# First ffn of an encoder layer: its first two hidden tiles by slices of channels, the first root's squares on VectorE, modulations as columns

## The chip, the cores and the metric

The kernel runs on one core of a Trainium2 chip. The metric is the device time in microseconds (us) of one execution. Names of the engines as in the profile: PE is TensorE (PEld its weight loads), DVE is VectorE, ACT is ScalarE, POOL is GpSimd, SP is SyncE, on whose queue nearly all loads are issued. Each engine runs its own instructions strictly in their order and waits for others by semaphores.

## The reference

A layer for 1024 tokens of 1024 channels: half a SwiGLU ffn, a mixer (latent attention and a recurrence), half an ffn again, a final norm. What this case touches is the beginning:

```python
c_act = jax.nn.silu(c)
mod = c_act @ w_mod[l] + b_mod[l]                  # 9 x 1024
sh1, sc1, gt1, ... = jnp.split(mod, N_MOD, axis=-1)
u = modulate(rmsnorm(h, ffn1_norm_g[l]), sh1, sc1) # u * (1 + scale) + shift
h = h + 0.5 * gt1[:, None, :] * swiglu(u, w_gate, w_up, w_down)
# rmsnorm: x * rsqrt(mean(x*x) + eps) * g;  swiglu: (silu(u @ w_gate) * (u @ w_up)) @ w_down
```

All in float32. The hidden width is 2816, 22 tiles of 128.

## The kernel before

Channels lie on the partitions, in 8 tiles of 128; tokens lie in the columns, in two halves of 512. `h[d][a]` is the stream's tile d in half a. A float32 product is made of three matmuls of a shorter type: each operand is split into a high part (a cast on ACT, L59) and a low part (a subtraction on DVE, L60), and `mm3` (L66) multiplies high by high, high by low, low by high. A pair of high and low part is called `pair` in the rows.

The opening of the first ffn is code in `tile_layer` and in `ffn`. `load_x` loads a half of the stream. `root(0)` squares the eight tiles on ACT and sums over channels on PE with a matrix of ones (L1644, L1645), so that the sum stands on every partition; `root_mean` (L252, L253) takes the square root on ACT and the reciprocal on DVE, 512 wide. `root(1)` goes by `SumSq` and `rstd`: squares on ACT, sums over tiles on DVE (L206, `nacc`), token sums on PE (L214), a root of four columns, and `spread` (L224, L228, L229), which lays it out on every partition, once in PSUM and once as a copy in SBUF (`nr`).

The shift and the gain of the first two tiles of channels are made on PE (`mod_first`, L150), as a row of 128 columns that is copied by ACT and turned into columns by small products (L158). Those of tiles 2 to 7 are made on DVE (`mod_one`, L138, twelve of them), each from a loaded weight tile `wmod` of 512 KB and the spread silu of c (`cact`). `gain` (L184) adds one and multiplies by the norm's weight.

`norm_raw` norms a tile: even tiles on DVE (L318) and then a shift on ACT (L319), odd tiles on POOL (L315) and then gain and shift on ACT (L316). Half 0 goes through `normed` and `stream_first`, half 1 through `second_half`.

The first two hidden tiles go by `up_plain`: 2 tiles x gate and up x 2 halves x 8 channel tiles x 3 = 192 matmuls (L66, sums `ps_w` in PSUM). All later ones go by seven products in place of eight (`products7`), for which `stream_sums` makes sums and differences of the two halves (L353) and splits them.

A scheduler puts every engine's instructions into an order when the program is built; the order of the code is its starting point. Short-lived tiles take slots in turn: `k.spare` (512 wide, squares) has four, `k.wide` (the `wmod` tiles) sixteen.

## Time and profile before

| | |
|---|---|
| time, median of 3 runs | 2127.43 us (2125.19 to 2128.57) |
| profiled execution, first to last instruction | 2127.5 us |
| PE, DVE, ACT, POOL busy | 96%, 73%, 43%, 12% |
| chain that ended last | PE 78%, DVE 13%, DMA 4%, others 5% |
| L66 products into `ps_w` (both ffns) | 3744, busy 876.8 us |

The profile has no other time for its execution than the span, which stands beside the median of the runs. The page is an overview; the rows below come from the timeline (start, duration, engine, line, operation, tiles, in brackets the idle time before it and what ended it), from windows (busy time of each engine in a stretch) and from groups (busy time and mean of a kind of instruction in a stretch).

### The profile page before, as it was taken

Reading aid. Unit: us, or ns where it says so; the run is one execution under the profiler, and the core shown is the slowest. Engines: PE = TensorE matmul, PEld = TensorE weight load, DVE = VectorE, ACT = ScalarE, POOL = GpSimd, SP = SyncE. Lnnn points to the kernel's source line nnn. Section 1 sums busy time; section 2 is a strip of 40 time slices with the busy share of each in tenths; the row PEclk is TensorE's granted clock in tenths of the full one; section 3 lists DMA queues with packets and bytes.
Section 4 is the critical chain, followed back from the end, with each engine's and each line's share of the span. In section 5 each row is a group of like instructions: output and inputs, shape, how many; then the busy total and the mean of one; then the engine's idle time right before and its main releaser. Section 6 shows DMA issues by size and latency. Waiting matters only on the chain.

```text
span 2127.5 us, 28417 instructions
## 1 busy us (share of the span) xinstructions
PE 2052.5 (96%) x10496; PEld 1649.7 (78%) x10496; DVE 1551.5 (73%) x2718; ACT 924.3 (43%) x1614; POOL 251.6 (12%) x259
## 2 busy tenths in 40 slices
PE   6999999999999999997989999999999999999998
PEld 4788878887888767766768887777888888878887
DVE  6999996579895677788865656566655556589975
ACT  5643343344342566652344443455433333454333
POOL 1100000000001254531142222111000000000001
PEclk8999999999999999999999999999999999999999
DMA  8277732235332124545336853551322222363322
GB/s 329 94 236 246 248 112 94 89 125 182 105 124 93 56 70 131 139 127 131 91 86 168 198 161 119 193 177 52 100 88 73 86 80 89 99 193 109 102 72 80
DMA packets 189771, 273.74 MB, mean 129 GB/s; under 512 B 77504, under 2 KB 121920, under 8 KB 189632
## 3 DMA queue, kind: packets, MB, share of 16 engines
q1 hardware_dynamic: 187920, 268.62, 40.5%
q0 software_dynamic: 1280, 3.15, 0.5%
q8 instruction: 83, 1.36, 0.3%
q14 instruction: 56, 0.46, 0.1%
q10 hardware_dynamic: 432, 0.15, 0.0%
HBM read 202.66 MB, written 66.58 MB: 127 GB/s over the span
## 4 chain that ended last, share of the span: by engine, by line
PE 78%; DVE 13%; DMA 4%; issue 2%; ACT 1%; SPq 1%; POOL 1%; DVEq 0%; ACTq 0%; POOLq 0%
PE ps_w L66 36%; PE ps_dn L66 20%; PE ps_in L66 5%; PE ps_wo L66 3%; DVE Tpr L1317 2%; DVE pair L60 2%; PE ps_ov L1230 2%; PE ps_z L1415 1%; PE ps_s L66 1%; PE ps_uq L66 1%; DVE T L1321 1%; PE ps_x L951 1%; PE ps_pt L1222 1%; PE ps_s L1198 1%; PE ps_y L1442 1%
## 5 line engine op out<-in xcount | busy, mean ns | idle before, releaser
L66 PE MATMUL ps_w<-pair 128*128 128x512 f32 x3744 | 876.8, 395 | 13.4 <-ACT pair L59 9.7
L66 PEld LDWEIGHTS ps_w<-pair 128*128 128x128 f32 x3744 | 704.7, 189 | 182.7 <-ACT pair L59 11.3
L66 PE MATMUL ps_in<-pair,win 128*128 128x512 f32 x960 | 253.2, 414 | 8.4 <-DVE acc L1069 4.1
L60 DVE TENSOR_TENSOR pair<-raw,pair 128x512 fp32r<-128x512 f32 x256 | 177.8, 703 | 109.0 <-ACT pair L59 108.9
L59 ACT CAST pair<-raw 128x512 fp32r<-128x512 f32 x256 | 155.4, 621 | 226.4 <-PE ps_w L66 178.4
L66 PE MATMUL ps_dn<-pair 128*128 128x512 f32 x1008 | 236.6, 393 | 3.1 <-DVE part L608 1.7
L66 PEld LDWEIGHTS ps_in<-pair,win 128*128 128x128 f32 x960 | 183.4, 194 | 59.2 <-issue 10.9
L66 PEld LDWEIGHTS ps_dn<-pair 128*128 128x128 f32 x1008 | 188.9, 188 | 47.9 <-DVE part L608 2.5
L66 PE MATMUL ps_dn<-pair,dh 128*128 128x512 f32 (+1 forms) x704 | 204.2, 375 | 0.0
L66 PEld LDWEIGHTS ps_dn<-pair,dh 128*128 128x128 f32 x704 | 128.1, 188 | 25.8 <-issue 0.7
L388 ACT COPY part<-ps_w 128x512 f32<-128x512 f32 x120 | 70.1, 585 | 166.6 <-PE ps_w L66 157.9
L66 PE MATMUL ps_dn<-pair,dl 128*128 128x512 f32 (+1 forms) x352 | 131.2, 375 | 0.0
L551 DVE SCALAR_TENSOR_TENSOR h<-ps_dn,mod,h 128x512 f32<-128x512 f32 (+1 forms) x128 | 90.6, 715 | 37.6 <-PE ps_dn L66 37.3
L59 ACT CAST pair<-hraw 128x512 fp32r<-128x512 f32 x124 | 73.4, 620 | 69.5 <-DMA hraw<-hidD 29.6
L206 POOL TENSOR_TENSOR nacc<-nacc,nsq 128x512 f32<-128x512 f32 x12 | 17.7, 1472 | 670.4 <-ACT nsq L202 670.4
L138 DVE SCALAR_TENSOR_TENSOR wmod<-wmod,cact 128x1024 f32<-128x1024 f32 x68 | 83.1, 1224 | 9.6 <-DMA wmod<-w_mod 9.3
L486 DVE TENSOR_TENSOR t<-ps_w,part 128x512 f32<-128x512 f32 x80 | 54.8, 691 | 46.5 <-PE ps_w L66 27.9
L60 DVE TENSOR_TENSOR pair<-hraw,pair 128x512 fp32r<-128x512 f32 x124 | 83.4, 689 | 5.9 <-ACT pair L59 5.6
L699 POOL TENSOR_TENSOR h<-h,nr 128x256 f32<-128x256 f32 (+1 forms) x6 | 5.4, 916 | 648.8 <-ACT nr L229 648.8
L66 PE MATMUL ps_wo<-pair,woh 128*128 128x512 f32 x256 | 80.0, 394 | 0.6 <-ACT woh L59 0.6
L66 PEld LDWEIGHTS ps_dn<-pair,dl 128*128 128x128 f32 x352 | 66.3, 188 | 12.9 <-issue 0.2
L481 DVE TENSOR_TENSOR c<-ps_w,part 128x512 f32<-128x512 f32 x80 | 53.5, 688 | 28.8 <-PE ps_w L66 23.5
(348 smaller groups left out, 3101.7 us busy)
## 6 DMA issues: line engine op xcount, KB each, us to landing
wmod<-w_mod SPq DMA_DIRECT2D x68, 512.0 KB, 4.4
raw<-ffn_w_gate SPq DMA_DIRECT2D x44, 512.0 KB, 3.6
raw<-ffn_w_up SPq DMA_DIRECT2D x44, 512.0 KB, 4.5
hidD<-c SPq DMA_DIRECT2D x44, 512.0 KB, 2.7
hraw<-hidD SPq DMA_DIRECT2D x44, 512.0 KB, 3.3
draw<-ffn_w_down SPq DMA_DIRECT2D x40, 512.0 KB, 3.7
h<-x SPq DMA_DIRECT2D x32, 256.0 KB, 4.8
hD<-h SPq DMA_DIRECT2D x32, 256.0 KB, 2.0
```

The lines of the kernel that those rows point to most:

```text
L59: k.nc.scalar.copy(out=hi, in_=src)
L60: k.nc.vector.tensor_tensor(out=lo, in0=src, in1=hi.bitcast(F32), op=ALU.subtract)
L66: k.nc.tensor.matmul(out, lhsT=x, rhs=y, start=start, stop=stop, skip_group_check=onto)
L138: k.nc.vector.scalar_tensor_tensor(out=w, in0=w, scalar=1.0, in1=k.cact, op0=ALU.mult, op1=ALU.mult, accum_out=m)
L388: nc.scalar.copy(out=t, in_=x)
L481: nc.vector.tensor_tensor(out=c[i][:, j], in0=x, in1=y, op=ALU.add)
L486: nc.vector.tensor_tensor(out=t, in0=x, in1=y, op=ALU.add)
L551: nc.vector.scalar_tensor_tensor(out=y, in0=x, scalar=gt[:, d : d + 1], in1=y, op0=ALU.mult, op1=ALU.add)
L951: nc.tensor.matmul(t[:, 2 * P * e : 2 * P * (e + 1)].rearrange("p (h s q) -> p h s q", s=2, q=L), lhsT=BK8[:, 2 * c + e, :], rhs=pad[:, 2 ...
L1198: nc.tensor.matmul(t[:, :mm], lhsT=r[high], rhs=k.kr[1, b][high, :mm], start=False, stop=True)
L1230: nc.tensor.matmul(x.po[:, cols], lhsT=pt[:, b * P : (b + 1) * P], rhs=k.v[b][:, cols], start=b == 0, stop=b == x.i)
L1317: nc.vector.tensor_tensor(out=v, in0=T[:, 0:t, 0:t].rearrange("p s c -> p c s"), in1=xp[:, 0:t, t][:, None, :].broadcast_to([P, t, t]), op ...
```

## The change

The first two hidden tiles of the first ffn go by `up_sliced`. It loads all four weight tiles first, then splits them, and takes the products by a table `SLICES` of (half, channel tiles, hidden tiles): tiles 0, 1 of half 0, tiles 2, 3 of half 0, tiles 0 to 3 of half 1 for the first hidden tile, and so on. A callback `feed(half, tile)` norms and splits a tile of the stream just before the first slice that needs it, and makes the second root when the first tile of half 1 is asked for. The first root goes the way of the second one (`SumSq` with sums on DVE, `rstd`). Both norms now take the root from its copy in SBUF. `mod_first` makes the columns directly, the weight tile as the stationary operand. `k.spare` has three slots, `k.wide` eight, and the second root's copy lies in the fourth slot.

```diff
 def mod_first(k, d, w):
     nc = k.nc
-    t = ps(k, "norm")
+    t = ps(k, "norm")[:, :2]
     for v in range(2):
         for i in range(ND):
             nc.tensor.matmul(
-                t[0:1, v * P : (v + 1) * P], lhsT=k.ccol[:, i : i + 1], rhs=w[v][:, i * P : (i + 1) * P],
+                t[:, v : v + 1], lhsT=w[v][:, i * P : (i + 1) * P], rhs=k.ccol[:, i : i + 1],
                 start=i == 0, stop=i == ND - 1,
             )
-    row = tmp(k, "row")[0:1, : 2 * P]
-    nc.scalar.copy(out=row, in_=t[0:1, : 2 * P])
-    t = ps(k, "norm")[:, :2]
-    for v in range(2):
-        nc.tensor.matmul(
-            t[:, v : v + 1], lhsT=row[:, v * P : (v + 1) * P], rhs=k.ones[0:1, 0:1], start=True, stop=True
-        )
...
+SLICES = (
+    (0, (0, 1), (0, 1)), (0, (2, 3), (0, 1)), (1, (0, 1, 2, 3), (0,)), (0, (4, 5), (0, 1)), (1, (4, 5), (0,)),
+    (0, (6, 7), (0, 1)), (1, (6, 7), (0,)), (1, tuple(range(ND)), (1,)),
+)
...
+    def up_sliced(f):
+        A, c = [], []
+        for i in range(2):
+            for w in (wg, wu):
+                raw = pool.tile([P, 2, HB], F32, name="raw", tag="raw", bufs=4)
+                nc.sync.dma_start(out=raw.rearrange("p a (d q) -> p (a d) q", q=P), in_=w[f + i])
+                A.append((raw, [pair(pool, "wo", 8) for _ in range(2)]))
+        start[0]()
+        for b in range(2):
+            for raw, blocks in A:
+                split(k, raw[:, b], *blocks[b])
+        c = [cell() for _ in range(2)]
+        sums, fed = {}, set()
+        for j, slices, which in SLICES:
+            for d in slices:
+                if (j, d) not in fed:
+                    fed.add((j, d))
+                    sliced(j, d)
+            for i in which:
+                for e in range(2):
+                    if (i, e, j) not in sums:
+                        sums[i, e, j] = ps(k, "w7")
+                    for d in slices:
+                        hi, lo = A[2 * i + e][1][d // 4]
+                        q = slice(d % 4 * P, (d % 4 + 1) * P)
+                        mm3(k, sums[i, e, j], hi[:, q], lo[:, q], *u["plain"][j][d], d == 0, d == ND - 1)
...
+        start[3]()
...
-        k.wide = spare(us)
-        k.spare = spare(fs[8:])
+        k.wide = spare(us[:8])
+        k.spare = spare(fs[8:11])
...
         def root(a):
-            if a:
-                ss = SumSq(k, pool, nc.vector)
-                for d in range(ND):
-                    ss.add(h[d][a])
-                r = rstd(k, pool, ss)
-                return r
-            t = ps(k, "norm")
+            ss = SumSq(k, pool, nc.vector)
             for d in range(ND):
-                sq = tmp(k, "nsq")
-                nc.scalar.activation(out=sq, in_=h[d][a], func=AF.Square)
-                nc.tensor.matmul(t, lhsT=k.ones, rhs=sq, start=d == 0, stop=d == ND - 1)
-            r = pool.tile([P, HB], F32, name="r", tag="nr", bufs=1)
-            root_mean(k, t, D, r)
-            return r, r
+                ss.add(h[d][a])
+            r.append([rstd(k, pool, ss, ("nr", "f11")[a])[1]] * 2)
...
+        def feed(a, d):
+            if a and not d:
+                root(1)
+            if not a and d >= early:
+                mods(d)
+            norm_raw(k, r[a], h[d][a], d, "ffn1_norm_g", 0)
+            split(k, h[d][a], *u["plain"][a][d])
```

How the built order changes, at three places. First ACT at the program's start, before; `raw` are weight tiles, `r` is the first root:

```order
L252 ACT_TABLE_LOAD
L252 ACTIVATE r_191<-ps_norm_166,eps_67 128x512
L59 CAST pair_244<-raw_242 128x512
L59 CAST pair_245<-raw_242 128x512
L155 COPY row_211<-ps_norm_194 1x256
L59 CAST pair_252<-raw_250 128x512
L59 CAST pair_253<-raw_250 128x512
L59 CAST pair_260<-raw_258 128x512
```

and with the change, where `nr_216` is the first root's copy:

```order
L245 ACT_TABLE_LOAD
L245 ACTIVATE rt_213<-ps_norm_204,eps_67 128x4
L59 CAST pair_261<-raw_259 128x512
L59 CAST pair_265<-raw_263 128x512
L59 CAST pair_269<-raw_267 128x512
L222 COPY nr_216<-ps_norm_218 128x512
L59 CAST pair_273<-raw_271 128x512
L59 CAST pair_262<-raw_259 128x512
```

The root of 512 columns stood ahead of all eight casts. Now a root of four columns stands there, and the copy of the spread root behind three casts.

Then DVE around the second root, before (`nr_420` is its spreading, `mod_77` the modulations, `pair_367` to `pair_369` tiles 5 to 7 of half 0, `raw_877` a weight tile of the next hidden tiles):

```order
L184 SCALAR_TENSOR_TENSOR gs_ffn1_norm_g_81<-mod_77,pv_140 128x1
L60 TENSOR_TENSOR pair_367<-h4_0_148,pair_367 128x512
L138 SCALAR_TENSOR_TENSOR wmod_314,mod_77<-wmod_314,cact_274 128x1024
L141 TENSOR_TENSOR mod_77<-mod_77,b_mod_141 128x1
L318 SCALAR_TENSOR_TENSOR h6_0_149<-h6_0_149,gs_ffn1_norm_g_81,r_191 128x512
L141 TENSOR_TENSOR mod_77<-mod_77,b_mod_141 128x1
L184 SCALAR_TENSOR_TENSOR gs_ffn1_norm_g_81<-mod_77,pv_140 128x1
L224 TENSOR_TENSOR nr_420<-ident_60,rt_417 128x512
L60 TENSOR_TENSOR pair_368<-h6_0_149,pair_368 128x512
L395 TENSOR_TENSOR s1_897<-raw_877 128x512
L60 TENSOR_TENSOR pair_369<-h6_0_149,pair_369 128x512
L374 TENSOR_TENSOR raw_877<-raw_875,raw_877 128x512
```

and with the change (`rt_444` is the second root before it is spread, which is the row after the last one here; `pair_146` is tile 6; `raw_744`, `s1_898`, `raw_878` belong to the next hidden tiles):

```order
L138 SCALAR_TENSOR_TENSOR wmod_305,mod_77<-wmod_305,cact_275 128x1024
L141 TENSOR_TENSOR mod_77<-mod_77,b_mod_157 128x1
L60 TENSOR_TENSOR pair_146<-h6_0_165,pair_146 128x512
L367 TENSOR_TENSOR raw_744<-raw_742,raw_744 128x512
L138 SCALAR_TENSOR_TENSOR wmod_315,mod_77<-wmod_315,cact_275 128x1024
L388 TENSOR_TENSOR s1_898<-raw_878 128x512
L141 TENSOR_TENSOR mod_77<-mod_77,b_mod_157 128x1
L177 SCALAR_TENSOR_TENSOR gs_ffn1_norm_g_81<-mod_77,pv_156 128x1
L246 RECIPROCAL rt_444<-rt_444 128x4
L141 TENSOR_TENSOR mod_77<-mod_77,b_mod_157 128x1
L367 TENSOR_TENSOR raw_878<-raw_876,raw_878 128x512
L177 SCALAR_TENSOR_TENSOR gs_ffn1_norm_g_81<-mod_77,pv_156 128x1
```

One sum (L388) and two differences (L367) of the next tiles' weights stand here ahead of the spreading, and another sum a few rows higher; the gain of tile 7 (the last row) stands directly before it.

Last PE at the passage from half 0 to half 1, before (`pair_368`, `pair_369` are tiles 6 and 7 of half 0; `pair_441`, `pair_442` tiles 0 and 1 of half 1):

```order
L66 MATMUL ps_w7_544<-pair_368,pair_269 128x512 x2
L66 MATMUL ps_w7_544<-pair_369,pair_269 128x512
L66 MATMUL ps_w7_466<-pair_369,pair_245 128x512 x2
L66 MATMUL ps_w7_491<-pair_369,pair_253 128x512 x2
L66 MATMUL ps_w7_519<-pair_369,pair_261 128x512 x2
L66 MATMUL ps_w7_544<-pair_369,pair_269 128x512 x2
L66 MATMUL ps_w7_571<-pair_441,pair_244 128x512
L66 MATMUL ps_w7_596<-pair_441,pair_252 128x512
L66 MATMUL ps_w7_571<-pair_441,pair_244 128x512 x2
L66 MATMUL ps_w7_571<-pair_442,pair_244 128x512
```

and with the change (`pair_146`, `pair_147` are tiles 6 and 7 of half 0; `pair_148`, `pair_149` tiles 0 and 1 of half 1):

```order
L66 MATMUL ps_w7_343<-pair_146,pair_262 128x512 x3
L66 MATMUL ps_w7_343<-pair_147,pair_262 128x512 x3
L66 MATMUL ps_w7_350<-pair_146,pair_266 128x512 x3
L66 MATMUL ps_w7_350<-pair_147,pair_266 128x512 x3
L66 MATMUL ps_w7_357<-pair_146,pair_270 128x512 x3
L66 MATMUL ps_w7_357<-pair_147,pair_270 128x512 x3
L66 MATMUL ps_w7_364<-pair_146,pair_274 128x512 x3
L66 MATMUL ps_w7_364<-pair_147,pair_274 128x512 x3
L66 MATMUL ps_w7_468<-pair_148,pair_261 128x512
L66 MATMUL ps_w7_481<-pair_148,pair_265 128x512
L66 MATMUL ps_w7_468<-pair_148,pair_261 128x512 x2
L66 MATMUL ps_w7_468<-pair_149,pair_261 128x512
```

In both orders the products of half 0 come before those of half 1. The spread of the second root stood ahead of tile 6's products and now stands ahead of tile 5's; with tile 5 (12 products) the rows of tiles 6 and 7 (24) are what is left of half 0 there.

## Rows read from the trace of the kernel before

**Rows 1.** Windows: us, busy us of PE, PEld, DVE, ACT, POOL, clock, DMA

```profile
20.00:30.00 10.00, 4.34 (x31) 3.22 (x30) 10.00 (x15) 5.96 (x9) 5.65 (x4) 0.75 1.03 400
...
40.00:50.00 10.00, 6.02 (x32) 4.77 (x30) 10.00 (x25) 4.83 (x8) 0.00 (x0) 0.78 0.70 276
...
70.00:80.00 10.00, 10.00 (x44) 8.04 (x43) 10.00 (x18) 8.63 (x16) 0.00 (x0) 1.00 0.00 0
```

**Rows 2.** Timeline, PE: start, us, instructions merged, idle before

```profile
65.58 34.78 PE L66 MATMUL ps_w<-pair 128*128 128x512 f32 x142 [2.03 <-DVE pair L60]
```

**Rows 3.** Groups of PE from 28.9 to 65.5: busy us, mean ns, idle before

```profile
L66 PE MATMUL ps_w<-pair 128*128 128x512 f32 x98 | 27.8, 439 | 10.0 <-ACT pair L59 9.7 <-DVE pair L60 0.2
```

**Rows 4.** Groups from 70 to 140

```profile
L66 PE MATMUL ps_w<-pair 128*128 128x512 f32 x304 | 70.6, 394 | 0.0
```

**Rows 5.** Timeline of the first root and the raw splits, 9 to 29

```profile
9.28 0.74 SPq L452 DMA_DIRECT2D raw<-ffn_w_gate  x1
...
10.10 0.63 ACT L1644 ACTIVATE nsq<-h 128x512 f32<-128x512 f32 x1 [0.23 <-PE ps_norm L1645]
...
13.58 1.28 ACT L252 ACT_TABLE_LOAD   x1 [2.85 <-PE ps_norm L1645]
...
15.60 3.35 DVE L253 RECIPROCAL r<-r 128x512 f32<-128x512 f32 x1 [15.60 <-ACT r L252]
...
18.87 2.30 DVE L60 TENSOR_TENSOR pair<-raw,pair 128x512 fp32r<-128x512 f32 x2
...
19.09 6.55 POOL L315 TENSOR_TENSOR h<-h,r 128x512 f32<-128x512 f32 x4 [17.08 <-DVE r L253]
...
21.16 3.36 DVE L60 TENSOR_TENSOR pair<-raw,pair 128x512 fp32r<-128x512 f32 x2
...
24.44 1.22 DVE L184 SCALAR_TENSOR_TENSOR gs_ffn_norm_g<-mod,pv 128x1 f32<-128x1 f32 x1
...
27.45 1.28 DVE L60 TENSOR_TENSOR pair<-raw,pair 128x512 fp32r<-128x512 f32 x2
```

**Rows 6.** Timeline of the second root, 42 to 57

```profile
42.86 0.28 PE L214 MATMUL ps_norm<-ones,nacc 128*128 128x1 f32 x2
...
44.34 0.36 PE L214 MATMUL ps_norm<-ones,nsq 128*128 128x1 f32 x2
...
44.73 0.26 ACT L252 ACTIVATE rt<-ps_norm,eps 128x4 f32<-128x4 f32 x1 [2.89 <-PE ps_norm L214]
...
54.02 0.69 DVE L224 TENSOR_TENSOR nr<-ident,rt 128x512 f32<-128x512 f32 x1
...
55.89 1.02 PE L228 MATMUL ps_norm<-nr,ones 128*128 128x512 f32 x2
```

**Rows 7.** Loads issued from 8.9 to 9.5: KB each, us to landing

```profile
raw<-ffn_w_gate SPq DMA_DIRECT2D x1, 512.0 KB, 10.3
```

**Rows 8.** Groups of DVE from 28.6 to 54

```profile
L138 DVE SCALAR_TENSOR_TENSOR wmod<-wmod,cact 128x1024 f32<-128x1024 f32 x12 | 14.6, 1221 | 0.0
L206 DVE TENSOR_TENSOR nacc<-nacc,nsq 128x512 f32<-128x512 f32 x6 | 4.1, 688 | 0.6 <-ACT nsq L202 0.4
L60 DVE TENSOR_TENSOR pair<-h,pair 128x512 fp32r<-128x512 f32 x6 | 4.1, 687 | 0.0
L318 DVE SCALAR_TENSOR_TENSOR h<-h,gs_ffn_norm_g,r 128x512 f32<-128x512 f32 x3 | 2.3, 750 | 0.0
```

**Rows 9.** Timeline of half 1's norm, 59 to 65

```profile
59.44 2.71 DVE L318 SCALAR_TENSOR_TENSOR h<-h,gs_ffn_norm_g,ps_norm 128x512 f32<-128x512 f32 x4
...
60.84 0.80 ACT L316 ACTIVATE h<-h,mod,gs_ffn_norm_g 128x512 f32<-128x512 f32 x1
...
62.07 2.85 DVE L353 TENSOR_TENSOR h<-h,h 128x512 f32<-128x512 f32 x3
62.16 0.60 ACT L59 CAST pair<-h 128x512 fp32r<-128x512 f32 x1
```

**Rows 10.** Window of the slow clock after the restart at 65.58

```profile
66.00:69.00 3.00, 3.00 (x9) 2.33 (x8) 3.00 (x6) 2.99 (x5) 0.00 (x0) 0.50 0.03 5
```

More of the change, by code (lines that the diff above doesn't have):

```diff
@@ L253, in root_mean, with rstd @@
     k.nc.vector.reciprocal(out=out, in_=out)
-def rstd(k, pool, ss):
+def rstd(k, pool, ss, tag="nr"):
     t = ps(k, "norm")
@@ L429, in ffn @@
 def ffn(
-    k, u, h, wg, wu, wd, gt, pool, groups, cells, start, turn, steps1, steps2, final, done, pieces, ahead=None
+    k, u, h, wg, wu, wd, gt, pool, groups, cells, start, turn, steps1, steps2, final, done, pieces, ahead=None,
+    sliced=None
 ):
```

36 lines of the change are left out of this document (15 added, 21 removed).

## The prediction

> **What bounds the kernel now.** I read the page first: PE is busy 96% of the span and has 78% of the chain that ended last. In the windows PE has no gap from about 70 us on [rows 1], so what the opening of the first ffn loses or wins is passed on whole to the end. In the same windows the opening itself: between 20 and 30 us PE is busy 4.34 us and between 40 and 50 it is 6.02, while DVE has 10.00 in both. PE waits there for what DVE prepares. PE's own timeline then tells where this ends: at 65.58 it starts to run without a gap [rows 2], and by then it has done 98 of the 192 products of the first two hidden tiles [rows 3]. DVE's order until then: it splits the raw weights, computes twelve modulations, norms half 0, sums the squares of half 1, makes the second root, norms half 1.
>
> The profiled execution spans 2127.5 us; the median of the runs is 2127.43. I add to 2127.5 and treat the two as one.
>
> **The measure.** A product that PE does in the gap-free stretch costs 70 us / 304 = 0.230 us [rows 4]. The end moves by the shift of the gap-free start, plus 0.230 us for each product that is then left to do and was done before.
>
> **Part 1, the first root.** Before: eight full-width products, then a square root, then a reciprocal of 3.35 us on DVE; the root is there at 15.60 + 3.35 = 18.95 [rows 5]. After: the last square ends at 10.73 as now at the earliest. Six sums on DVE of 0.69 us (the same operation in the second root, [rows 8]) run beside the squares; from the third square on they are a chain, and I let it end at 11.4. Token sums as in the second root, 44.34 + 0.36 - 42.86 = 1.8, then its root of four columns 0.26, the spreading 0.69 on DVE and 1.02 on PE [rows 6], and the table load 1.28 [rows 5]: 16.5 to 17. But nobody reads it there. Both uses now take the copy in SBUF, and ACT, in order, makes this copy behind three casts of raw weights. The third raw tile is issued at 9.28 [rows 5] and lands 10.3 us later [rows 7], at 19.6. With the cast and the copy at 0.60 each [rows 9] the root is there at 20.8, not 2 us earlier but 1.85 later. Without that landing it would be there at 17.5, 1.5 earlier; I take the landing, since the load queue ahead of it is unchanged.
>
> **Part 2, the modulations as columns.** 32 products of one column replace 32 of 128 columns, four small ones and two round trips over ACT. By the second root, where 8 such products take 1.8 us, 32 take 7.4. PE has 5.7 us idle between 20 and 30 [rows 1], and by part 3 DVE reads the first result after 24. I cost it at nothing; at twice the time it would end at about 29 and still wait for DVE.
>
> **Part 3, DVE up to the first norm.** While POOL multiplies four tiles, from 19.09 for 6.55 us, two splits take 3.36 us in place of 1.28, and a gain of one column 1.22 [rows 5]. After, POOL starts at 20.8 and ends at 27.4. Three splits are done before that; three more and the gain go at POOL's pace until 27.4; the last two take 1.28 and the norm 0.75: 29.4. Before, the same set (eight splits, the norm, two small ones) was done at 28.7. So +0.7.
>
> **Part 4, DVE from there to the second root.** Before: 28.7 to 54.02 [rows 6], 25.3 us with 0.6 idle, so 24.7 of work: twelve modulations of 1.22, six sums, six splits, three norms, small ones [rows 8]. The order of the change puts the same set there and four operations of the next tiles more (two sums and two differences, 0.60 each): +2.4. And two splits now stand directly behind what ACT must first deliver: tile 3's waits about 0.4, tile 4's follows its own norm, so DVE waits for a shift and a cast, 0.80 + 0.60 [rows 9]. On the load queue the eight slots of `wmod` let the next tiles' four raw loads ahead of the last six modulation tiles, but the bytes are the same: at 400 GB/s the 276 of the slice from 40 to 50 end at 46.9 [rows 1], and DVE asks for the last two tiles after 53. The second root is spread at 29.4 + 24.7 + 2.4 + 0.4 + 1.4 = 58.3, with the last gain directly before it, in place of 54.0.
>
> **Part 5, PE.** All 96 products of half 0 still stand ahead of those of half 1; the slices do not make the halves alternate on PE. Tile 5 of half 0 is cast on ACT behind the shift of tile 7, which needs the last gain. From 58.3: two shifts of 0.80 and two casts of 0.60 make 61.1. PE has then done the 60 products of tiles 0 to 4 and waits; before, at 65.58, it had done 98. From 61.1 on the 36 products left of half 0 take 8.3 us. Both restarts follow a wait and run at first at a granted clock of 0.50, 1.2 GHz: 9 products in 3 us [rows 10] where 13 would go. This is in both and cancels.
>
> The sum: (61.1 - 65.58) + (98 - 60) x 0.230 = -4.5 + 8.7 = **+4.2**.
>
> **Part 6, half 1 behind it.** The copy of the second root is there at about 61.7. Before, DVE took this root from PSUM: four norms in 2.71 us beside POOL, while three sums from SBUF, started beside POOL, took 2.85 in place of 1.9 [rows 9]. After, the norms read SBUF too. At POOL's pace of 6.55 us for four they end at 68.3, and the first split of half 1, behind three sums, at 70.8; at PSUM's pace at 66.9. PE asks for it after its 36 products, about 1 us of slow clock and two products that need the cast alone: 61.1 + 8.3 + 1.0 + 0.5 = 70.9. So at POOL's pace this wait is just covered. I add 0.3 for it: **+4.5, 2132.0 us**. What is lost there beyond that goes to the end whole; if PSUM's pace held, nothing of the 4.2 would change.
>
> The Trainium skill, SBUF — State Buffer, section Who interferes with whom, says that a VectorE instruction with two SBUF inputs contends with a GpSimd instruction that reads SBUF, and that one with a single SBUF input does not. The rows agree: 0.66 us for a norm from PSUM beside POOL, 1.68 for a split. By it the norms of part 6 lose 3.9 us behind that cover; without it the cover has 3.9 us to spare and the sum is 4.2.
>
> **The rivals.**
>
> *Not slower: POOL falls into DVE's waits.* Three splits are done before POOL starts. If the rest went at 0.6 us each, DVE would reach the modulations at 26.4, when the spread c is there, and not at 29.4; the last gain comes at 55.3, PE restarts at 58.1, and the end moves by 4.2 - 3.0 = +1.2, which is no change to be told. It decides where the first modulation on DVE starts before 27. For it: ACT's casts come one by one, so DVE has idle time. Against it: at the same place two splits took 3.36 us.
>
> *Slower still: the second sums come late.* The change leaves ACT three slots for squares in place of four, so the fifth square of half 1 waits for DVE's first sum, about 35.9 (29.4, four modulations, a split, the sum), and tile 1's cast stands four shifts and casts and three squares behind it, at 41.6; its split ends at 44.5. Then 32 products of tiles 1 to 3 stand ahead of the second sums. At 0.230 us they end near 52, and DVE asks for the root near 58: 3.5 us to spare after sums and root. If PE kept the low clock of [rows 10] through all of them they would take 14.7 us; the sums end near 61.5, ACT's root holds up the shifts behind it, and PE restarts near 65: +8. For it: every restart here begins slow. Against it: none stayed so for over 7 us.
>
> *The later order gives or takes.* Names and order move on DVE, ACT and the load queue in places up to the output projection, partly where DVE and not PE is the chain (13% of it). The runs of before lie 3.4 us apart; I allow 6 us either way, the side of a faster kernel included. It decides only if the gap at the first ffn's end is not the one at the program's end.
>
> *It does not do what it says.* That the halves do not alternate on PE is in the sum already. If half 1's products did fill the wait before tile 5, some 38 products less would be left and the result would be 4.2 - 8.7 = -4.5; PE's order speaks against it.
>
> **How the numbers follow.** About 0.2%, 4.3 us, is what a measurement of this kernel tells from no change. The forecast, +4.5 with a range of its own of +2 to +8 (no landing wait in part 1 below; more waits in parts 4 and 6 above): 0.60. POOL in DVE's waits, +1.2: 0.15. Late sums, +8: 0.13. Later order, -6 to +6 on top: 0.12. Slower by over 4.3: a little over half of the forecast, the late sums and half of the later order, 0.52. Faster by over 4.3: the far side of the later order, 0.07. Within: 0.41. The range 2127.3 to 2137.5 holds the forecast's own range and the values of two rivals, and leaves out the far sides of the last.
>
> **What would show it.** Right: the first root's copy ends near 20.8, behind a cast that waits for its load; the first modulation on DVE starts near 29.4; the second root is spread near 58.3; PE restarts near 61.1 behind a cast, with 60 products done, and has no gap after about 72. Wrong: products of half 1 before the last of half 0; splits of 0.6 us beside POOL; PE waiting for DVE after 72; gaps after 200 us that were not there. A restart at 56.8 with 60 products done would make the kernel as fast as before, and an earlier one faster.

## The result and the profile after

The changed kernel takes 2144.57 us (median of four runs, 2141.49 to 2145.34) against 2128.00 (four runs, 2125.19 to 2130.57): a ratio of 1.0078, 95% interval 1.0066 to 1.0091. It is slower, as forecast, but by far more: 2132.0 was forecast, and 2137.5 was the range's upper end.

The profiled execution spans 2143.6 us, 16.1 more than before. Where they go is read from four starts on PE that both traces have: the first product into `ps_dn` (the ffn's second part), into `ps_in` (the projection's early products), into `ps_lora` (its later ones), and the end.

| | to first ps_dn | to first ps_in | to first ps_lora | to the end |
|---|---|---|---|---|
| before | 468.1 | 237.4 | 54.3 | 1367.7 |
| after | 476.6 | 239.0 | 59.9 | 1368.1 |
| difference | +8.5 | +1.6 | +5.6 | +0.4 |

So there are two places: the opening, and a stretch of 60 us at 715 to 775 us, of which the forecast knew nothing.

**The opening.** The windows that answer to [rows 1]:

```profile
20.00:30.00 10.00, 10.00 (x43) 8.97 (x42) 5.73 (x6) 5.52 (x8) 5.61 (x4) 1.00 1.03 399
40.00:50.00 10.00, 5.73 (x13) 3.64 (x12) 8.12 (x17) 5.88 (x11) 0.00 (x0) 1.00 0.67 265
70.00:80.00 10.00, 9.09 (x40) 7.03 (x39) 10.00 (x16) 9.91 (x17) 1.19 (x1) 1.00 0.01 2
```

From 20 to 30 us PE is now the full engine, and DVE waits. (The clock of 1.00 in the first two rows is not to be believed: see the last section.) PE's timeline, which answers to [rows 2] and [rows 6], says what fills it:

```profile
11.62 0.56 PE L207 MATMUL ps_norm<-ones,nacc 128*128 128x1 f32 x2 [11.62 <-DVE nacc L199]
...
14.60 0.56 PE L207 MATMUL ps_norm<-ones,nsq 128*128 128x1 f32 x2
16.86 4.85 PE L150 MATMUL ps_norm<-ccol,wmod 128*128 128x1 f32 x22 [1.69 <-ACT rt L245]
21.58 2.05 PE L221 MATMUL ps_norm<-nr,ones 128*128 128x512 f32 x2
23.42 8.96 PE L150 MATMUL ps_norm<-ccol,wmod 128*128 128x1 f32 x42
34.05 2.08 PE L66 MATMUL ps_w<-pair 128*128 128x512 f32 x4 [1.67 <-ACT pair L59]
...
58.31 0.36 PE L207 MATMUL ps_norm<-ones,nsq 128*128 128x1 f32 x2
...
64.17 9.13 PE L66 MATMUL ps_w<-pair 128*128 128x512 f32 x38 [0.18 <-ACT pair L59]
74.20 6.09 PE L66 MATMUL ps_w<-pair 128*128 128x512 f32 x25 [0.91 <-DVE pair L60]
```

A token sum of the first root takes 0.56 us, one of the second 0.36. The columns (the modulations of `mod_first`, L150) wait 1.69 us: they take the PSUM bank from which ScalarE still reads the token sums. Eleven of the 32 (two records each) then run ahead of the first root's spread. The other engines, against [rows 5], [rows 6] and [rows 9]:

```profile
16.54 0.26 ACT L245 ACTIVATE rt<-ps_norm,eps 128x4 f32<-128x4 f32 x1
...
17.12 0.69 DVE L217 TENSOR_TENSOR nr<-ident,rt 128x512 f32<-128x512 f32 x1
...
19.19 0.62 ACT L59 CAST pair<-raw 128x512 fp32r<-128x512 f32 x1 [0.65 <-DMA raw<-ffn_w_gate]
...
23.67 0.58 ACT L222 COPY nr<-ps_norm 128x512 f32<-128x512 f32 x1 [3.86 <-PE ps_norm L221]
...
31.86 0.74 DVE L311 SCALAR_TENSOR_TENSOR h<-h,gs_ffn_norm_g,nr 128x512 f32<-128x512 f32 x1
...
62.07 0.68 DVE L217 TENSOR_TENSOR nr<-ident,rt 128x512 f32<-128x512 f32 x1
...
64.84 6.90 DVE L311 SCALAR_TENSOR_TENSOR h<-h,gs_ffn_norm_g,nr 128x512 f32<-128x512 f32 x4
```

The spread's operand is ready at 17.81; PE takes it up at 21.58; the copy is there at 24.25. From the first norm on DVE has hardly a wait up to the second root. Its groups from 31.8 to 62.1, against [rows 8], show the four added operations, 2.8 us:

```profile
L138 DVE SCALAR_TENSOR_TENSOR wmod<-wmod,cact 128x1024 f32<-128x1024 f32 x12 | 14.4, 1215 | 0.0
...
L388 DVE TENSOR_TENSOR s<-raw 128x512 f32<-128x512 f32 x2 | 1.4, 682 | 0.0
L367 DVE TENSOR_TENSOR raw<-raw 128x512 f32<-128x512 f32 x2 | 1.4, 678 | 0.0
```

PE is free of gaps from 74.20, with the same 98 products done as before at 65.58. Most of the 8.6 us between these starts can be read off DVE: its first modulation starts at 32.52 where it started at 28.72 (+3.8); from there to the start of the second root's spreading it takes 29.55 us where it took 25.30 (+4.25); the rest is PE's.

**The stretch at 760 us.** PE and ACT after:

```profile
744.59 17.91 PE L66 MATMUL ps_in<-pair,win 128*128 128x512 f32 x69 [0.67 <-DVE pair L274]
765.10 1.74 PE L66 MATMUL ps_in<-pair,win 128*128 128x512 f32 x4 [2.59 <-ACT win L59]
```

```profile
752.35 0.58 ACT L841 COPY raw<-ps_in 128x512 f32<-128x512 f32 x1
762.54 1.56 ACT L841 COPY raw<-ps_in 128x512 f32<-128x512 f32 x3 [9.61 <-PE ps_in L66]
763.98 1.07 ACT L59 CAST win<-win 128x1024 fp32r<-128x1024 f32 x1
```

and ACT before, at the same place:

```profile
742.09 1.07 ACT L805 COPY raw<-ps_in 128x512 f32<-128x512 f32 x2
749.03 0.59 ACT L805 COPY raw<-ps_in 128x512 f32<-128x512 f32 x1 [5.87 <-PE ps_in L66]
750.20 0.59 ACT L805 COPY raw<-ps_in 128x512 f32<-128x512 f32 x1 [0.58 <-PE ps_in L66]
750.68 1.05 ACT L59 CAST win<-win 128x1024 fp32r<-128x1024 f32 x1
```

The second copy, whose product is long done, now waits 9.6 us for another product of PE; the cast of the next weights stands behind it on ACT, and PE waits 2.59 us for the cast. Afterwards it runs at a granted clock of 0.66 in the mean of five us:

```profile
764.00:769.00 5.00, 3.61 (x9) 2.40 (x10) 3.92 (x3) 3.36 (x5) 4.32 (x5) 0.66 0.20 32
```

ACT has the same instructions in the same order at this place in both kernels. What differs is where tiles lie. The changed kernel claims 16 split tiles (asks the pools for their places in SBUF) at its start, and the first ffn's other tiles move up in SBUF. The projection's shifted tiles `raw` take memory that the ffn gives back. In the built program the second one now begins 32 bytes before the end of weights that the third early product (`ps_in2`) reads last, and its copy waits for the last of these reads.

### The profile page after: what moved, and what is told of

Same layout as the page of the kernel before. It is cut to its first block, busy times and chain, and to the rows that moved or that the text cites. A ratio compares the mean times of both kernels' runs of the same rounds, so it can differ in the third digit from the quotient of the medians.

```text
span 2143.6 us, 28419 instructions
## 1 busy us (share of the span) xinstructions
PE 2061.5 (96%) x10490; PEld 1658.7 (77%) x10490; DVE 1560.6 (73%) x2725; ACT 922.2 (43%) x1613; POOL 248.8 (12%) x259
## 4 chain that ended last, share of the span: by engine, by line
PE 70%; DVE 17%; DMA 6%; issue 4%; ACT 2%; SPq 1%; POOL 1%; DVEq 0%; ACTq 0%; POOLq 0%
PE ps_w L66 27%; PE ps_dn L66 20%; PE ps_in L66 5%; PE ps_wo L66 4%; DVE pair L60 3%; DMA wmod<-w_mod 3%; DVE wmod L138 2%; DVE Tpr L1353 2%; PE ps_ov L1266 2%; PE ps_z L1451 2%; PE ps_s L66 1%; DVE T L1357 1%; PE ps_y L1478 1%; PE ps_pt L1258 1%; PE ps_s L1234 1%
## 5 line engine op out<-in xcount | busy, mean ns | idle before, releaser
L66 PE MATMUL ps_in<-pair,win 128*128 128x512 f32 x960 | 259.4, 421 | 13.5 <-ACT acc L1099 4.3
L199 POOL TENSOR_TENSOR nacc<-nacc,nsq 128x512 f32<-128x512 f32 x12 | 17.5, 1461 | 670.1 <-ACT nsq L195 670.0
```

Of the source, the lines that this page charges most:

```text
L66: k.nc.tensor.matmul(out, lhsT=x, rhs=y, start=start, stop=stop, skip_group_check=onto)
```

## The experiments

The theory: the loss at 760 us comes of the tiles' places alone; that of the opening comes of the first root, which PE spreads late and slowly, and of half 1's norms from SBUF. The rivals: the changed order of instructions, and DVE's chain of work whatever the root does. Every edit makes the scheduler deal out instructions anew, except where it is said that the order stayed. The letters (theory L, rival O and so on) are those of the expectation that stands with each run. All times:

| kernel | us, median | ratio to before, interval | to ps_dn | to ps_in | to ps_lora | to end |
|---|---|---|---|---|---|---|
| e1_layout | 2140.94 | 1.0060 [1.0046, 1.0073] | 475.2 | 240.2 | 55.1 | 1368.0 |
| g1_claims | 2129.16 | 1.0002 [0.9991, 1.0013] | 467.6 | 237.5 | 54.2 | 1365.3 |
| h1_under | 2132.47 | 1.0014 [1.0004, 1.0024] | 468.1 | 237.9 | 59.3 | 1365.3 |
| e4_bank | 2146.28 | 1.0084 [1.0069, 1.0100] | 482.9 | 238.9 | 55.5 | 1367.3 |
| f2_spread | 2143.54 | 1.0069 [1.0057, 1.0081] | 478.5 | 241.3 | 55.1 | 1366.6 |
| e3_warm | 2151.09 | 1.0103 [1.0087, 1.0119] | 488.6 | 242.0 | 59.3 | 1362.5 |
| f4_warm44 | 2141.08 | 1.0066 [1.0052, 1.0079] | 486.5 | 238.9 | 54.4 | 1361.2 |
| e2_psum | 2146.90 | 1.0082 [1.0067, 1.0096] | 475.1 | 242.6 | 58.4 | 1370.7 |
| f1_both | 2142.93 | 1.0060 [1.0047, 1.0074] | 473.2 | 238.3 | 54.3 | 1374.6 |
| f3_slices_psum | 2133.49 | 1.0022 [1.0014, 1.0031] | 474.2 | 238.5 | 54.7 | 1364.6 |
| e5_rows | 2147.03 | 1.0081 [1.0065, 1.0098] | 482.5 | 237.5 | 54.9 | 1372.4 |
| e6_root | 2142.85 | 1.0061 [1.0044, 1.0078] | 481.2 | 238.8 | 54.9 | 1368.9 |
| e7_noslice | 2144.54 | 1.0065 [1.0047, 1.0083] | 483.6 | 240.7 | 54.4 | 1368.8 |
| e8_slices | 2135.76 | 1.0034 [1.0022, 1.0047] | 476.4 | 238.1 | 54.6 | 1369.2 |
| g2_before3 | 2131.90 | 1.0005 [0.9996, 1.0014] | 472.7 | 237.4 | 55.3 | 1365.8 |
| g3_slices3 | 2132.56 | 1.0012 [1.0003, 1.0022] | 468.8 | 237.7 | 53.1 | 1368.6 |
| g3_slices4 | 2139.88 | 1.0049 [1.0035, 1.0063] | 474.8 | 238.4 | 54.7 | 1374.5 |

The segments are those of the one profiled execution, and those of one order differ by some 2 us without a cause in the edit. The changed kernel, e1_layout, e2_psum and f1_both have the same products from 84 us to the first `ps_dn`, without a wait and at a granted clock of 1.00; for the same 1680 records in that stretch PE took 391.6, 390.2, 391.3 and 389.4 us. Why is not known. Each ratio is to the kernel before on the same chip.

### The places in SBUF

**e1_layout**, against the changed kernel; same order on every engine:

```diff
-        u = {"plain": [[pair(*s) for s in fs[:8]], [pair(*s) for s in us[8:]]]}
...
+        u = {"plain": [[], []]}
...
+            u["plain"][a].append(pair(*(fs[:8], us[8:])[a][d]))
             split(k, h[d][a], *u["plain"][a][d])
...
```

> The changed kernel, but the split tiles of the first ffn's input are claimed from their pools one by one when they are fed, as the kernel before claims them, instead of all at the start; the order of the instructions on every engine stays that of the changed kernel. Theory L (memory): the changed kernel's early claims push the ffn's other tiles along in SBUF, so that the second of the projection's shifted tiles (raw) comes to lie over weights that the last early products read; its copy waits until 762.5, ACT's cast of the next weights stands behind it, TensorE waits 2.6 us for that cast and then runs at half clock. Then the copies go at 752, the 2.6 us wait falls under 0.5, the distance between the first ps_in and the first ps_lora shrinks from 59.9 to about 54.5 us, and the time is 2138 to 2140. Rival O (order): the 5.6 us lost between 705 and 765 us come of the products being dealt out in another order there; then nothing changes: distance 59.9, time 2144 to 2145. Both: gap-free start of TensorE stays at 74.2.

ACT and PE of e1_layout:

```profile
752.04 1.07 ACT L841 COPY raw<-ps_in 128x512 f32<-128x512 f32 x2
...
760.63 1.05 ACT L59 CAST win<-win 128x1024 fp32r<-128x1024 f32 x1
```

```profile
744.29 26.25 PE L66 MATMUL ps_in<-pair,win 128*128 128x512 f32 x105 [0.66 <-DVE pair L274]
```

Two copies go at once, the cast follows 3.4 us earlier, PE has no gap, and the segment is 55.1 instead of 59.9. PE's gap-free start stayed where it was, at 74.24. Theory L held, with the time 1 us above its range. The medians fell by 3.6 us; their intervals still overlap.

**g1_claims**, against the kernel before; same order on every engine:

```diff
...
-        u = {}
+        u = {"plain": [[pair(*s) for s in fs[:8]]]}
...
```

> The kernel before, with one thing taken from the change: the first half's eight split tiles are claimed from their pool at the start instead of where they are first written. No instruction is added, removed or moved on any engine; only the places of the first ffn's tiles in SBUF change. Theory L (memory): the shifted tiles of the projection come to lie over weights that the last early products of the projection read, ScalarE's first copy waits for these products, and the next weights' cast behind it comes late for TensorE. Then the distance between the first ps_in and the first ps_lora grows from 54.3 to 57 to 60 us and the time to 2130 to 2134, while the first ps_dn stays at 468 to 469. Rival O (the 5 us came with the order of the changed kernel): distance 54 to 55, time 2126 to 2130.

These are rival O's numbers: 54.2, and no change of time. They don't speak for its cause, though. The claims had moved the tiles, but weights of the second product (`ps_in1`) came to lie under the shifted tiles, and ACT's copies, which waited for that product to end at 748.2, lost nothing, since the third copy waits for it anyway. The edit had missed the condition that it was to test.

**h1_under**, against the kernel before; again the same order on every engine:

```diff
...
-        u = {}
+        u = {"plain": [[pair(*s) for s in fs[:8]]]}
+        for tag in ("cact", "h6_1", "e"):
+            pool.tile([P, D], F32, name=tag, tag=tag)
...
```

> The kernel before with the same instructions in the same order on every engine; eight split tiles and three more places of the first ffn are claimed early. In g1_claims the early claims put the shifted tiles over weights of another product, which ends at 748 us anyway, and nothing was lost. With the three further claims the second shifted tile (raw) lies over weights that the third early product (ps_in2) reads, as in the changed kernel. Theory L (the tiles' places alone make the loss at 760 us): the second copy waits for the end of ps_in2 at about 752, ScalarE's cast of the next weights comes at 753.5 instead of 750.7, TensorE waits 2 to 3 us for it and then runs at half clock for some us; the distance between the first ps_in and the first ps_lora is 57.5 to 60 us instead of 54.3, and the time 2131 to 2134. Rival O (it takes the changed kernel's order as well): distance 54 to 55.5, time 2127 to 2130.

ACT and PE of h1_under:

```profile
752.45 1.56 ACT L806 COPY raw<-ps_in 128x512 f32<-128x512 f32 x3 [1.50 <-PE ps_in L66]
753.89 1.07 ACT L59 CAST win<-win 128x1024 fp32r<-128x1024 f32 x1
```

```profile
755.01 10.39 PE L66 MATMUL ps_in<-pair,win 128*128 128x512 f32 x31 [2.59 <-ACT win L59]
```

The wait of 2.59 us is there, to the hundredth, in the kernel before, without one instruction moved: 59.3 instead of 54.3. Theory L is shown. Of the 5.0 us lost here some 3 are left at the end (1.0014 [1.0004, 1.0024]). The other kernels agree: the segment is 58.4 to 59.9 in the changed kernel, e2_psum and e3_warm, where a copy has to wait for `ps_in2`, and 53.1 to 55.5 in all that don't. Among these are e4_bank and f4_warm44, which claim the 16 tiles early too: there the weights under the shifted tiles are those of `ps_in1`. So it is not the early claim by itself that costs, but whose weights come to lie there.

### The first root

**e4_bank**, against the changed kernel:

```diff
-    t = ps(k, "norm")[:, :2]
+    t = ps(k, "modf")[:, :2]
...
-    banks(k, w7="012345", norm="67", dn="67")
+    banks(k, w7="012345", norm="67", dn="67", modf="54")
```

> The changed kernel, but the first modulations' columns have two banks of PSUM of their own (4 and 5, free until the products need them) instead of taking turns with the norm's two. Theory B (bank): the columns no longer wait 1.7 us for ScalarE's square root to have read the token sums; they start at 15.2, those ahead of the spread end by 18 to 18.5, the spread runs at 18 to 20.5 and the first root's copy is there at 20.7 to 21.3 instead of 24.25; gap-free start 71 to 72.5, time 2141 to 2143 unless the later order moves it. Rival (the modulations' chain on VectorE, not the root, sets the first half): the copy comes early but the first products stay within 0.5 us of 34.05 and the gap-free start of 74.2.

The columns started at 14.96, but 13 of them went ahead of the spread; it ran at 20.50, and the copy came at 23.83, 0.4 us earlier. The first products came 3.1 us earlier, at 30.98; the gap-free start did not: the moved rows put the second sums in place of products, and the first `ps_dn` came 6.3 us later. Theory B got its wait removed and not its gain.

**f2_spread**, against f1_both (below):

```diff
         root(0)
+        next(k.bank["norm"])
         for d in range(early):
             mods(d)
```

> The same as the one with both edits, and the two banks of the norm change places for the first modulations, so that four columns instead of eleven stand ahead of the first root's spread. Theory S (the columns ahead of the spread hold the first root up): the spread runs at 17.9 to 20.5 instead of 21.6 to 23.6, the root's copy is there at 20 to 21.5 instead of 24.25, the first products start at 30.5 to 32 instead of 34.05, and the products of half 0 end 2 to 3 us earlier; time 2135 to 2139, unless the rows that move after it cost some us. Rival D (VectorE's splits and modulations set the first products): the copy comes at 20 to 21.5, but the first products stay at 33 to 34.5 and the time at 2138 to 2141.

PE and ACT of f2_spread:

```profile
18.77 2.05 PE L221 MATMUL ps_norm<-nr,ones 128*128 128x512 f32 x2
20.62 11.95 PE L150 MATMUL ps_norm<-ccol,wmod 128*128 128x1 f32 x56
42.16 5.54 PE L66 MATMUL ps_w<-pair 128*128 128x512 f32 x16 [9.60 <-ACT pair L59]
```

```profile
20.87 0.59 ACT L222 COPY nr<-ps_norm 128x512 f32<-128x512 f32 x1 [2.00 <-PE ps_norm L221]
```

With four columns ahead of it the spread runs at 18.77 and the copy is there at 21.46: the columns do hold up the root, by 2.8 us. But the first products came at 42.16, 8 us later, since DVE's and ACT's rows had been dealt out anew, and `ps_dn` 5.3 us later than in f1_both. What an early root is worth with all else equal could not be measured: no edit of it left the order alone.

**e3_warm** and **f4_warm44** (WARM = 24 and 44), against the changed kernel:

```diff
+        warm = ps(k, "warm")
+        for _ in range(WARM):
+            nc.tensor.matmul(warm[:, :P], lhsT=k.ones, rhs=k.ones, start=True, stop=True)
         vectors(k, pool)
```

> The changed kernel, plus 24 matmuls 128x128 of ones by ones into a bank that nothing reads, at the very start, while TensorE has nothing else to do. Theory C (slow clock): TensorE, idle up to 11.6 us, does the eight token-sum pairs in 3.5 us and the spread in 2.05 us at half speed; kept busy before, it does them in 1.8 to 2 and 1.05 us and the modulation columns in 0.11 us each, the first root's copy moves from 24.25 to 20 to 21, and the gap-free start from 74.2 to 70.5 to 72; time 2141 to 2142.5 unless the order later gives or takes some us. Rival W (the waits set it): the matmuls run at the same 0.56 us a pair, the first root's copy stays at 24 to 24.5 and the time at 2143 to 2146.

> The changed kernel plus 44 instead of 24 matmuls of ones by ones at the start, so that TensorE is busy until about 11 us and not only until 8.2. With 24 the token sums after 3.2 us without work ran at a granted clock of 0.50 and 0.56 us a pair. Theory C (the clock falls in the wait, and that makes the sums slow): with no wait ahead of them the eight pairs run at 0.28 to 0.36 us each, 1.8 to 2 us in all, the columns at 0.11 us each, the spread in 1.05 us, and the first root's copy comes at 19.5 to 21.5 instead of 24.1. Rival W (matmuls of one column take 0.56 us a pair there whatever the clock): as with 24, 0.56 us a pair and a copy at 23.5 to 24.5. The time, 2143 to 2152, says little: the order of the rows behind is another than the changed kernel's.

e3_warm kept PE busy until 8.2 us, and then it waited 3.2. The copy came at 24.1, as rival W had it, and the time, with another order behind, is the longest of all. Windows of PE with the granted clock third from the end, and a token sum:

```profile
4.20:8.00 3.80, 3.80 (x36) 1.00 1.00 350
...
11.60:13.10 1.50, 1.50 (x8) 0.50 1.02 418
```

```profile
11.89 0.56 PE L207 MATMUL ps_norm<-ones,nsq 128*128 128x1 f32 x2
```

In f4_warm44 PE had no wait ahead of the sums:

```profile
13.10:15.00 1.90, 1.85 (x18) 1.00 1.02 414
15.00:16.60 1.60, 0.00 (x0) 0.72 1.03 402
16.70:21.50 4.80, 4.80 (x23) 0.50 1.03 412
```

```profile
13.47 0.36 PE L207 MATMUL ps_norm<-ones,nacc 128*128 128x1 f32 x2
```

So 0.56 us is the same sum at 1.2 GHz and 0.36 at 2.4, and eight take 1.84 us instead of 3.54: the first half of theory C. The second half fell. Behind the sums of one column, in the columns' wait of 1.69 us, the clock went down again; the columns, of which 14 and not 11 now stood ahead of the spread, and the spread were slow as before, and the copy came at 25.3 and not at 20.

### Half 1's norms

**e2_psum**, against the changed kernel; same order on every engine:

```diff
-            r.append([rstd(k, pool, ss, ("nr", "f11")[a])[1]] * 2)
+            got = rstd(k, pool, ss, ("nr", "f11")[a])
+            r.append(got if a else [got[1]] * 2)
```

> The changed kernel, but VectorE's four norms of half 1 read the root from PSUM, as the kernel before does (GpSimd's four still read the SBUF copy). Theory N (the four norms go at GpSimd's pace because both read SBUF): VectorE's four take 2.7 to 3 us instead of 6.9, the products of half 1 start about 2 us earlier, the waits of 0.9 and 1.35 us for VectorE's splits go, and the gap-free start moves from 74.2 to about 72; time 2142 to 2143. Rival (the splits wait for GpSimd's tiles anyway): the four get short but the gap-free start stays within 0.5 us of 74.2 and the time at 2144 to 2145. The later loss at 760 us stays in both.

DVE and PE of e2_psum:

```profile
64.81 2.72 DVE L311 SCALAR_TENSOR_TENSOR h<-h,gs_ffn_norm_g,ps_norm 128x512 f32<-128x512 f32 x4
```

```profile
64.14 14.25 PE L66 MATMUL ps_w<-pair 128*128 128x512 f32 x60 [0.18 <-ACT pair L59]
...
506.31 12.95 PE L66 MATMUL ps_dn<-pair 128*128 128x512 f32 x47 [3.13 <-ACT part L638]
```

Theory N: 2.72 instead of 6.90 us, and no wait for DVE behind the restart. Of the 4.2 us DVE keeps half: GpSimd is at work until 70.3, and the three sums behind the norms now take 3.97 us, mostly beside it, instead of 1.88, so that the first splits of half 1 come at 71.33 and not at 73.47. PE is 1.2 us ahead at 84 us, less than the 2 expected, and 1.5 at the first `ps_dn`. The time did not follow. At 503 us PE waited 3.13 us for an operation behind weights that landed late, where the changed kernel waited 1.0 in two parts; the order is the same, but three loads of `x` took SP 6.1 us to issue instead of 4.8. Theory N is right on the place, and its gain is smaller than what such a later place gives or takes.

**f1_both**: both edits, same order.

> The changed kernel with both single edits together: split tiles claimed as they are fed, and VectorE's four norms of half 1 from PSUM; the order of the instructions is the changed kernel's. Theory A (the two losses are separate and add): against the claims alone (first ps_dn 475.2, 2140.9 us) the norms give back 1.5 to 2 us: first ps_dn 473 to 474, time 2138 to 2140. Rival H (what is gained in the opening is lost where the second half of the ffn is handed over, at 495 to 515, by weights that land later): first ps_dn 473 to 475, but the distance from there to the first ps_in, 237.4 us before and 240.2 with the claims alone, grows to 242 or more and the time stays at 2140 to 2143.

`ps_dn` came at 473.2, inside theory A's range; the time did not. Rival H fell (238.3). But part of that is luck: against e1_layout PE is 1.3 us ahead at 84 us, as with the single edit, and the other 0.8 of the 2.0 us came in the stretch where nothing was changed. And 6.6 us more than in e1_layout went between the first `ps_lora` and the end, where the order is the same too. All of that and a little more lies at 1138 to 1154 us, in the recurrence: the same 100 records of PE took 16.0 us there, and 8.3 in e1_layout. PE of f1_both, then the same window (busy us of PE, PEld, DVE, ACT, POOL, clock, DMA) of f1_both and of e1_layout:

```profile
1143.25 0.77 PE L1451 MATMUL ps_z<-sv,m 128*64 128x64 f32 x5 [2.73 <-DMA sv<-vD]
```

```profile
1144.00:1155.00 11.00, 11.00 (x85) 9.29 (x82) 4.28 (x16) 4.02 (x11) 1.27 (x1) 0.50 0.70 176
```

```profile
1144.00:1155.00 11.00, 11.00 (x142) 9.32 (x141) 6.71 (x30) 5.82 (x17) 1.27 (x1) 1.00 0.59 131
```

In f1_both PE waited there for a load and then did its small products at half clock; e1_layout has no such wait. Both are busy for all of these 11 us, with 85 records against 142. Why the load came late is not known.

### The parts undone

All four are against e1_layout. **e5_rows** puts back `mod_first` of the kernel before, **e6_root** its first root, **e8_slices** both; **e7_noslice** undoes the slices:

```diff
-            ... (more_loads, None, None, both), ... ahead, feed,
+            ... (more_loads, lambda: [feed(a, d) for a in range(2) for d in range(ND)], lambda: None, both), ... ahead,
```

> The changed kernel with the split tiles claimed as they are fed (2140.9 us by itself, split tiles' opening ends with the first ps_dn at 475.2) and the first modulations computed as rows again, as in the kernel before. Theory S (the new first root is what comes late, the columns cost nothing of their own): rows, too, run on a slow TensorE and 12 of them stand ahead of the spread as 11 columns did, so the first root's copy stays at 23 to 25.5 and the time at 2139 to 2142. Rival K (the columns, 32 matmuls of 128 weights for one column each, hold the first half up): the copy comes at 20 to 21.5 and the time falls to 2136 to 2138.

> The same with the columns kept and the first root made as in the kernel before: the squares of half 0 summed by TensorE with a matrix of ones, root and reciprocal on all partitions. Theory S (the new first root is what comes late): TensorE is kept busy from 5 us and runs at full speed, the root is there at 19 to 19.5 instead of 24.25, the first products start at 29.5 to 31 instead of 34.05, the second root's spread at 58.5 to 60 instead of 62.9, first ps_dn at 470 to 472.5, time 2134 to 2138. Rival D (VectorE's own work, not the first root, sets the second root): the spread stays at 62 to 63 and the time at 2140 to 2142.

> The same with the new first root and the columns kept, but the slices undone: both halves are fed and the first two tiles' products go half by half as in the kernel before. Theory S (the late first root carries through): the root's copy at 24 to 24.5, the second root's spread at 57 to 59.5 (before 54.0, later by the 3 us that the first root loses), first ps_dn at 471 to 473, time 2131 to 2135. Rival V (the slices are what costs): first ps_dn at 468 to 469.5 and time 2127 to 2129. Rival G (the slices gain and the rest loses more): first ps_dn above 476, time above 2141.

> The slices alone: first root and modulation rows as in the kernel before, split tiles claimed as they are fed. Theory S: as with the old root alone, root at 19 to 19.5, second spread at 58 to 60, first ps_dn at 470 to 472.5, time 2131 to 2136, that is, slower than before by the work that the slices put ahead of the second root on VectorE and by the norms of half 1 from SBUF. Rival G (the slices by themselves gain, since products of half 0 fill TensorE's wait): first ps_dn under 467.5, time under 2127.

No theory held in the times. The first `ps_dn`, 475.2 in e1_layout, came at 482.5 without the columns, 481.2 without the new root, 476.4 without both, 483.6 without the slices. Parts that each look like a gain of 6 to 8 us, and two of them together like one of 1, do not add: each kernel is another schedule. Half of theory S for e5_rows was seen: the copy came at 23.6. In e6_root the first products came at 29.40 and the second spread at 57.5, somewhat ahead of what theory S expected, but PE then waited 4.6 and 5.0 us: an early root alone was no gain there. The slices alone cost 7.2 us [4.7, 10.0] by e8_slices' ratio; in e8_slices PE waits 7.14 us for half 1:

```profile
65.13 2.07 PE L66 MATMUL ps_w<-pair 128*128 128x512 f32 x4 [7.14 <-ACT pair L59]
```

**f3_slices_psum**: e8_slices with e2_psum's edit, same order.

> The slices alone (2135.8 us: first root and modulation rows as in the kernel before, split tiles claimed as they are fed), with VectorE's four norms of half 1 from PSUM as in the kernel before; order as in the slices alone. Theory N (the norms from SBUF beside GpSimd are what the slices pay): VectorE's four take 2.7 us, TensorE's wait of 7.1 us for half 1's first split falls to 4 to 5.5 us, first ps_dn at 473 to 474.5 instead of 476.4, time 2132 to 2135. Rival P (the first split of half 1 is a GpSimd tile's or stands behind modulations): the wait stays over 6.5 us and the time at 2135 to 2137.

The wait stayed at 7.14 with DVE's norms fast, as rival P had it; that a tile of POOL is first there is its reading. The next wait fell from 1.39 to 0.35 (theory N). `ps_dn` came 2.2 us earlier, of which 0.4 were there at the first products, ahead of the edit.

### DVE's chain, and a version that might win

**g2_before3** is the kernel before, **g3_slices3** and **g3_slices4** are f3_slices_psum, with `early = 3` (or 4) in place of 2.

> The kernel before, with the third tile's shift and gain computed by TensorE too (three tiles as rows instead of two). It takes two of the twelve 1.2 us products of the modulations, and their small additions, off VectorE and puts 16 matmuls of 0.23 us on TensorE, which waits there anyway. Theory V (VectorE's chain of modulations, squares and splits sets the second root and with it TensorE's restart): the second root's spread comes 2 to 3 us earlier than before's 55.9, the first ps_dn at 465 to 466.5, time 2124.5 to 2126.5. Rival T (TensorE's work or the loads set it): first ps_dn at 467.5 to 470, time 2127 to 2130.

> The slices with the old first root, rows, and half 1's norms from PSUM (2133.5 us), and the third tile's modulations on TensorE too. Theory V (as it stands, the slices only change what VectorE does before the second root, and TensorE then waits 7.1 us for half 1): with 2.7 us less on VectorE the wait falls to 3.5 to 5.5 us, first ps_dn at 470.5 to 472.5 instead of 474.2, time 2130 to 2132.5. Rival T: the wait stays at 6.5 to 8 us, first ps_dn at 473.5 to 476, time 2132.5 to 2137.

> The slices with old first root, rows and half 1's norms from PSUM, and four tiles' modulations on TensorE. With three the first ps_dn came at 468.8, 5.4 us earlier than with two, and the time was 2132.6. Theory V (VectorE's chain before the second root): another 2.7 us off it brings the first ps_dn to 465.5 to 467.5 and the time to 2127 to 2131, at or under the kernel before. Rival T (TensorE's rows now stand ahead of products that are ready, and the fourth tile's weights land late): first ps_dn at 468 to 471, time 2131 to 2135.

In the sliced opening three tiles moved the second root's copy from 58.2 to 53.5 us and `ps_dn` by 5.4, more than the 2.7 taken off DVE. In the kernel before the same edit made `ps_dn` 4.6 later, and four tiles in the sliced one 6.0 later than three. g2_before3's time agrees with no change [0.9996, 1.0014]. The chain is not the bound in general; theory V holds in one schedule of three. None of the versions beats the kernel before; the nearest sliced one, g3_slices3, is 0.12% slower [0.03, 0.22].

## Why the prediction was wrong

**Part 1 failed.** The copy of the first root was to be there at 20.8 and was at 24.25. The landing that was to hold it up came as said (casts at 17.92 and 19.19 behind a DMA) and was not what ended last. Against the 17.5 that Part 1 gives without the landing, the sums took 3.5 and not 1.8 (+1.7), since their duration was taken from the second root, where PE runs at a granted clock of 1.00; the spread stood 3.8 us behind columns; and it took 2.05 and not 1.02 (+1.0). That is 6.5 of the 6.75 us. f4_warm44 shows the sums' part: at a granted 1.00 they take 1.84.

**Part 2 failed with it.** "I cost it at nothing" looked only at when DVE reads the result. It did bound the columns' duration at twice 7.4, and 13.8 it was; what it did not look at is what stands between them on PE (the first root's spread), and for which bank they wait. f2_spread shows it: fewer columns ahead, copy 2.8 us earlier.

**Parts 3 to 6 were right in their steps and near in their sizes.** From the copy to the first norm's end 8.35 us (forecast 8.6); from there to the start of the second root's spreading on DVE 29.5 (28.9), with the four operations and a wait of 1.44 for tile 4; 2.1 more to the restart (2.8), with the 60 products done; the norms from SBUF 6.90 us (6.55), and a wait of 0.9 behind them (0.3). The 38 products behind the restart took 10.0 us with that wait, where 9.0 were forecast with one of 0.3. 3.45 for the copy and -0.25, 0.6, -0.7 and 1.0 for these make the 4.1 us between the forecast +4.5 and the measured 74.20 - 65.58 = 8.6; that the last four partly cancel is luck.

The Trainium skill, SBUF — State Buffer, section Who interferes with whom, says that a VectorE instruction with two SBUF inputs contends with a GpSimd instruction that reads SBUF, and that one with at most one, outside the 2-port perf modes, does not. The changed kernel and e2_psum agree: beside GpSimd a norm takes 1.72 us with both inputs in SBUF and 0.68 with one of them in PSUM.

**The measure failed in its assumption.** "Passed on whole to the end" left out that a change of claims moves tiles that are used 700 us later. That is 5.6 of the 16.1 us in the profile, e1_layout and h1_under show it, and no step or rival named it. How much of it reaches the end is less certain: 3.6 us in e1_layout's median, some 3 in h1_under's. The rival of the later order allowed 6 us but gave the cause to names and order; at this place the order did not change. The assumption held for the opening: 8.6 us at the gap-free start, 8.5 at the first `ps_dn`.

**The rivals.** POOL did not fall into DVE's waits: the first modulation came at 32.52, and beside POOL two splits took 3.10 us. The second sums were done at 58.7, 2.6 us before DVE's reciprocal at 61.26. (The forecast's 14.7 us for 32 products at the low clock takes twice 0.230 for each; the 9 in 3 us of [rows 10] make 10.7.) The halves did not alternate.

**Open**: what the late root costs at the end with all else equal, as every edit of the root also moved other rows; the 3.45 us are read from the one trace, and e6_root, with an early root, was not faster. Open too is why a load of the recurrence lands later in one execution than in another of the same order.

## What to carry to other kernels

Claiming a tile earlier is a change for every pool that later lies over the same memory: where pools are given back and taken again, compare which reader stands under the first tiles of the next stage. Take the duration of a small operation from a row with the same clock history, and count what stands ahead of it on its own engine, even if nobody waits for that. Where a scheduler deals out the instructions, an edit that keeps the order (here of claims or of an operand) tells more than one that undoes a part.

## What the runs showed of the hardware

The profile of the changed kernel gives the granted clock as 1.00 from 11.6 to 32 us, though a sum took 0.56 us there; e3_warm, where PE had worked before, gives 0.50 for the same 0.56. So the clock that this profile shows early in the execution, ahead of its first recorded change, is not to be relied on.

In e6_root PE did the columns from 14.76 without a gap, behind products of 512 columns, and the clock fell all the same; windows of PE there:

```profile
14.80:18.00 3.20, 3.20 (x29) 0.93 1.03 419
18.00:22.00 4.00, 4.00 (x20) 0.50 1.03 410
```

The rows of the kernel before, the same work in 128 columns, kept the short duration to their end:

```profile
13.43:16.90 3.47, 3.47 (x33) 1.00 1.03 420
```

So here PE fell to 1.2 GHz without having waited, after it had gone over from products of 512 columns to products of one: 11 us for the 32 columns of e6_root against 7.3 for the rows. That the width is the cause is not shown; the two kernels differ there in the weights too.
